# Reordering side work in a hybrid attention and retention layer: stores of f32 rows, operand sums, and the preparation of the output weights

## The chip, the cores and the metric

The kernel runs on one core of a Trainium2 chip. The metric is the device time of one execution in microseconds (us). The engines are TensorE (PE; its weight loads are shown apart as PEld), VectorE (DVE), ScalarE (ACT), GpSimd (POOL) and SyncE (SP), which here only issues DMAs. Each engine works through its own instructions in the order in which they stand in the program.

## What is computed

One layer over 2048 latent tokens and 256 context tokens of width 1024:

```python
h_lat = rmsnorm(x) * norm_g * (1 + scale) + shift        # the same for ctx, with its own scale and shift
na_q, na_k, na_v, na_g, r_q, r_k, r_v, r_g = split(h_lat @ w_in)       # w_in is 1024 x 4096
y_na  = neighbourhood_attention(na_q, na_k, na_v, context k and v, rpb) * silu(na_g)
y_ret = head_rmsnorm(retention(rotary(r_q), rotary(r_k), r_v)) * silu(r_g)
x = x + gate * (concat(y_na, y_ret) @ w_out)             # scale, shift, gate = silu(c) @ w_ada + b_ada
return rmsnorm(x) * final_norm_g
```

All is in f32. The kernel splits each f32 operand into a rounded part ("hi", tiles named hhi, whi) and the rest ("lo", hlo, wlo), and makes one product out of three matmuls: hi x hi, hi x lo, lo x hi.

## The kernel before, in words

The latent tokens are four blocks of 512 (0 to 3), the context is block 4. Weights are taken in columns of 256. The program runs through these stages, one after the other.

**Windows.** `window(b)` for b = 0 to 4 makes the attention keys of block b in 32 steps (a step is three matmuls, or the part of a unit up to its next `yield`). Beside them a table, PLAN, says at which step each piece of the norm and modulation of a later block runs: `squares`, `colsum`, `rstd`, `spread`, `spread_mul` (L241), `prep_ab` (scale and shift in place, L272 and L274) and `prep_hl` (hi on ACT at L279, lo on DVE or POOL at L283). The modulated f32 rows of blocks 0 to 3 are also stored to DRAM, in hS, because blocks 2 and 3 are loaded again later: `prep_hl` puts a pair (i, u) into the list `spill`, and `spill_step` (L253), called at every odd step, issues one store on SP's queue. SP's queue also holds the loads of x (L190), of ctx and of weights (L176) and the stores of the keys kS (L150). An entry of SP that waits holds up what is behind it.

**Context units.** Four units over CTXU (retention k and v of the context), then two for the attention values of the context. A unit is 48 matmuls of 128x256 (L377). Ahead of each, `w_split` (L348 on ACT, L350 on POOL for the first half of the weight and on DVE for the second) splits the weight of the *next* unit.

**First values.** Eight units `u_v` for blocks 0 and 1: each result is copied out of PSUM by ACT (L415) and DVE (L416) and stored by eight DMAs (L425). In the fourth and later units `w_sums` makes the first weights of the stage that follows.

**Round one.** `strassen` over SETS, six column sets for blocks 0 and 1 together, with seven products (L702) in place of eight. Its operands are sums of the blocks' halves (T, made by `h_sums`, ten parts: two each of `first`, `second`, `third`, then four of `fourth`) and sums of the weights' halves (`w_sums`). A set has four `step`s; a list `hooks` of 24 functions gives each step its side work.

**Second values, round two.** The same for blocks 3 and 2: `take` loads their f32 rows from hS into lo tiles (L842), `re_split` makes hi (L519) and lo (L520), and `h_sums_raw` makes the sums: `open_b` first, then nine parts. The units are two of block 3, two of block 3 with the second weight, then four of block 2. The parts of `h_sums` and `h_sums_raw` are not tied to a stage: `unit` pops one from `pump["q"]` after every `pump["every"]` steps.

**Output weights.** The gate row is the sum of eight pieces of w_ada (`wo_gate`, L768 on DVE, one 512 KB load each into `wraw`, L765), spread over the partitions by `wo_row` (four small matmuls, L775). `wo_mul` multiplies half of a 128-row piece of w_out by it (L780 on DVE), splits it (L782 on ACT, L783 on POOL; the tile `g` exists once) and stores both parts to woS from ACT's queue (L785).

**Attention, then retention and the output projection.** Not touched by the change. While attention runs, `fill` puts further projection units (L377, results at L452) between its steps.

What sets the order around the change is thus written by hand: PLAN, the order of appending to `spill`, the numbers of `pump`, and the indices of `hooks`.

Of the kernel before, what the change touches and what calls it, by code (L numbers as in the profile page):

```python
# [82 lines left out]
def hybrid_kernel(ctx: ExitStack, tc: tile.TileContext, a: dict, out: bass.AP):  # L83
# [160 lines left out]
        s, u, q = int(i == 8), k // 2, k % 2  # L244
        return scl[u][:, q, s:s + 1], mod[u][:, 0, q, s:s + 1]

    spill = []

    def spill_step():
        if spill:  # L250
            i, u = spill.pop(0)
            o = i % 2 * 256
            nc.sync.dma_start(hS[i // 2][:, u * KH:(u + 1) * KH, o:o + 256], raw[i][u])  # L253

    def prep_first(k):
        if k == KC - 1:
            spill.extend((i, u) for i in range(2) for u in range(2))
# [18 lines left out]
    def prep_hl(i, u):  # L276
        hi, lo = sub_dst(i)
        x, ks = raw[i][u], slice(u * KH, (u + 1) * KH)
        nc.scalar.copy(hi[:, ks, :], x)  # L279
# [214 lines left out]
    def window(b):  # L494
        units = [u_k(w01, 512 + 256 * g, ct, b) for g in range(2) for ct in range(2)]
        left = [KC] * 4
        for n, u in enumerate(STEPS if b == 0 else [u for u in range(4) for _ in range(KC)]):
            if b == 4 and n == 16:
                wr.append(w_split(wr[2]))
            next(units[u])  # L500
            left[u] -= 1
            run_acts(32 * b + n)
            if n % 2:
                spill_step()
            if not left[u]:
                for _ in units[u]:
                    pass
                tick()
# [16 lines left out]
    def h_sums_raw(T, A, B):  # L525
# [7 lines left out]
        def cast(key, c, d):  # L533
            nc.scalar.copy(t[key][:, 0, pairs(c), :], d)
# [10 lines left out]
            for n in (0, 2, 1, 3):  # L545
                re_split(B, pairs(n), (V, G)[n // 2])

        def a():
            tile_(3, "hlo")
            for c in range(2):  # L550
                cast(3, c, d(c))
            for c in range(2):
                low(3, c, d(c), (V, G)[c])

        def b():
            tile_(2, "hhi")
            for c in range(2):
                V.tensor_tensor(d(c), d(c), xa[:, pairs(c), :], ALU.add)
                cast(2, c, d(c))

        def first(c):
            if c == 0:
                e[0], e[1] = env["st"].tile([P, 2, 512], F32, name="o3", bufs=1), wo["p"].tile([P, 2, 512], F32, name="e")
            V.tensor_tensor(e[c], hb[:, pairs(c), :], xa[:, pairs(c), :], ALU.subtract)
            V.tensor_tensor(e[c], e[c], lb[:, pairs(c), :], ALU.add)
            low(2, c, d(c), (V, G)[c])

        def c_():
            tile_(4, "hlo")
            for c in range(2):  # L570
                V.tensor_tensor(d(c), xa[:, pairs(c + 2), :], d(c), ALU.subtract)
                cast(4, c, d(c))

        def raw_a(m):
            for n in (m, m + 2):
                re_split(A, pairs(n), (V, G)[n // 2])
            low(4, m, d(m), (G, V)[m])

        def last(c):
            if c == 0:  # L580
                tile_(1, "hhi")
                T.extend(t[n] for n in (1, 3, 2, 4))
            cast(1, c, e[c])
            low(1, c, e[c], (V, G)[c])

        return open_b, [a, b, lambda: first(0), lambda: first(1), c_, lambda: raw_a(0), lambda: raw_a(1), lambda: last(0), lambda: last(1)]

    def h_sums(T, A, B):
        (ah, al), (bh, bl) = ((f(x) for x in blk[b]) for b in (A, B))
# [270 lines left out]
    W, mine = values(vunits([(mid, 1024, 3), (w1, 1280, 3), (mid, 1024, 2), (w1, 1280, 2)]),  # L860
                     {0: [lambda: w1.append(w_split(wcur.pop(0), lo=1)), load_w, load_w], 1: [lambda: wo_gate(7)], 7: [wo_row]}, 5)
# [768 lines left out]
```

## Time and profile before

| | us |
|---|---|
| median of three runs | 1410.24 (1408.56 to 1411.27) |
| the profiled execution, whole | 1406.78 |
| its span, first to last instruction | 1405.0 |
| PE busy in the span | 1325.7 (94%) |
| DVE, POOL, ACT busy | 833.4, 654.2, 606.8 |
| mean granted TensorE clock | 0.985 |

The profile is one execution. In its views a row of the timeline gives the start, the duration, the engine, the line, the operation, out<-in by the names of the tiles, the shapes and a count; in brackets stands how long the engine was idle before it, and what ended that. A row of the windows gives, for one stretch of time, the busy time of each engine with the number of its instructions, then the mean granted clock of TensorE (1.00 is full), the share of the DMA engines that was busy, and GB/s. A row of the groups gives the busy time and the mean duration in ns of all instructions of one line and operation.

### The profile page before, as it was taken

The page shows a single profiled execution, that of the slowest core. Times are in us where ns is not written, and L with a number is a line of the kernel's source. Part 1 is how long each engine was busy: PE and PEld are TensorE (multiplying, and loading weights), DVE is VectorE, ACT ScalarE, POOL GpSimd, SP SyncE. Part 2 cuts the span into 40 slices and gives each one's busy share as a digit, 9 for nine tenths or more (in the row PEclk, how much of TensorE's full clock was granted, in tenths as well). Part 3 has the DMA queues.
Part 4 walks back from the last instruction along what each step waited for, and adds up shares of the span by engine and source line. Part 5 has one row for each costly group of instructions (what it writes and reads, how often), then busy time and mean ns, then how long its engine had stood idle before and what let it go on. Part 6 is the DMA issues. An engine that isn't in the chain of part 4 may idle for free.

```text
span 1405.0 us, 23114 instructions
## 1 busy us (share of the span) xinstructions
PE 1325.7 (94%) x8236; PEld 1161.0 (83%) x8236; DVE 833.4 (59%) x1422; ACT 606.8 (43%) x1261; POOL 654.2 (47%) x603
## 2 busy tenths in 40 slices
PE   6988979999879999899999999899999999999997
PEld 2567979988778878898899899798999779888886
DVE  5786364466673656267766777677663543344445
ACT  5453332233343344265556455565562234333332
POOL 4451445355444566355355455656343155454342
PEclk9999989999989999999999999999999999999999
DMA  9685636654655566895776788857636998555433
GB/s 320 206 275 190 207 123 172 159 186 152 247 160 138 189 241 218 256 242 162 203 195 198 187 253 209 212 159 204 174 114 214 272 309 270 187 171 168 157 113 128
DMA packets 233301, 278.86 MB, mean 198 GB/s; under 512 B 17121, under 2 KB 180065, under 8 KB 232162
## 3 DMA queue, kind: packets, MB, share of 16 engines
q1 hardware_dynamic: 201858, 221.01, 54.3%
q10 hardware_dynamic: 31328, 56.37, 11.1%
q8 instruction: 66, 1.08, 0.3%
q14 instruction: 49, 0.40, 0.1%
HBM read 188.19 MB, written 89.13 MB: 197 GB/s over the span
## 4 chain that ended last, share of the span: by engine, by line
PE 65%; DMA 8%; DVE 8%; POOL 7%; issue 6%; ACT 4%; SPq 2%; ACTq 1%; POOLq 0%; DVEq 0%
PE mm L377 16%; PE mm L1474 11%; PE mm L702 10%; PE mm L366 7%; PE sS L1034 4%; PE tr L1061 3%; PE po L1082 3%; PE mm L1197 2%; DMA hlo<-hS 2%; PE tr L1063 2%; PE po L1084 1%; DMA woS<-g 1%; PE mm L314 1%; POOL hlo L520 1%; DMA v<-rvS 1%
## 5 line engine op out<-in xcount | busy, mean ns | idle before, releaser
L377 PE MATMUL mm<-whi,hhi 128*128 128x256 f32 x768 | 227.6, 296 | 8.3 <-ACT hhi L519 4.6
L377 PE MATMUL mm<-whi,hlo 128*128 128x256 f32 x768 | 220.5, 287 | 8.2 <-DVE hlo L520 5.7
L377 PE MATMUL mm<-wlo,hhi 128*128 128x256 f32 x768 | 219.9, 286 | 1.6 <-POOL wlo L350 1.6
L1065 ACT CAST pt<-tr 128x640 fp32r<-128x640 f32 (+1 forms) x128 | 95.7, 747 | 162.4 <-PE tr L1063 156.9
L1071 DVE TENSOR_TENSOR pt<-tr,pt 128x640 fp32r<-128x640 f32 (+1 forms) x128 | 113.9, 890 | 80.5 <-ACT pt L1065 79.3
L377 PEld LDWEIGHTS mm<-whi,hlo 128*128 128x128 f32 x768 | 149.7, 195 | 9.6 <-DVE hlo L520 6.6
L377 PEld LDWEIGHTS mm<-whi,hhi 128*128 128x128 f32 x768 | 149.4, 194 | 9.2 <-ACT hhi L519 5.2
L1054 POOL TENSOR_SCALAR sp<-sp,stt 128x640 f32<-128x640 f32 (+2 forms) x128 | 103.1, 808 | 107.9 <-DVE stt L1053 78.4
L377 PEld LDWEIGHTS mm<-wlo,hhi 128*128 128x128 f32 x768 | 149.3, 194 | 1.8 <-POOL wlo L350 1.8
L1043 DVE CUSTOM_DVE_ANT_0 sp<-sS,nb 128x640 f32<-128x640 f32 (+2 forms) x128 | 105.5, 824 | 36.2 <-PE sS L1034 29.6
L1048 ACT ACTIVATE sp<-sp,stt 128x640 f32<-128x640 f32 (+2 forms) x128 | 107.4, 839 | 20.7 <-DVE stt L1043 19.6
L350 POOL TENSOR_TENSOR wlo<-st,whi 128x256 fp32r<-128x256 f32 (+1 forms) x79 | 83.6, 1069 | 59.2 <-ACT whi L348 48.3
L366 PE MATMUL mm<-hhi,whi 128*128 128x512 f32 x256 | 107.7, 421 | 0.0
L366 PE MATMUL mm<-hlo,whi 128*128 128x512 f32 x256 | 101.5, 397 | 5.6 <-DVE hlo L283 2.3
L1034 PE MATMUL sS<-k,q 128*128 128x256 f32 (+3 forms) x512 | 99.1, 315 | 5.8 <-DVE stt L1043 5.6
L366 PE MATMUL mm<-hhi,wlo 128*128 128x512 f32 x256 | 101.7, 397 | 0.2 <-DVE wlo L350 0.2
L702 PE MATMUL mm<-hhi,whi 128*128 128x512 f32 x336 | 98.4, 395 | 1.5 <-POOL whi L656 1.3
L1474 PE MATMUL mm<-wor,y 128*128 128x512 f32 x384 | 95.7, 398 | 1.2 <-DVE xt L1483 1.1
L1483 DVE TENSOR_TENSOR xt<-mm,xt 128x512 f32<-128x512 f32 x64 | 43.8, 686 | 84.7 <-PE mm L1474 84.6
L1034 PEld LDWEIGHTS sS<-k,q 128*128 128x128 f32 x512 | 82.7, 188 | 12.8 <-DVE stt L1043 9.1
L1474 PE MATMUL mm<-won,y 128*128 128x512 f32 x336 | 89.9, 406 | 0.0
L656 POOL TENSOR_TENSOR wlo<-st,wlo 128x512 fp32r<-128x512 f32 x36 | 51.5, 1432 | 79.7 <-ACT wlo L655 74.9
(274 smaller groups left out, 3159.3 us busy)
## 6 DMA issues: line engine op xcount, KB each, us to landing
st<-in_w_in_dram SPq DMA_DIRECT2D x64, 512.0 KB, 6.4
q<-qS SPq DMA_DIRECT2D x64, 256.0 KB, 4.4
k<-kS SPq DMA_DIRECT2D x16, 576.0 KB, 9.3
kS<-o SPq DMA_DIRECT2D x16, 512.0 KB, 3.5
vB<-o SPq DMA_DIRECT2D x64, 128.0 KB, 2.1
qS<-o ACTq DMA_DIRECT2D x16, 512.0 KB, 6.2
hlo<-hS SPq DMA_DIRECT2D x16, 512.0 KB, 7.7
woS<-g ACTq DMA_DIRECT2D x32, 256.0 KB, 3.3
```

The lines of the kernel that those rows point to most:

```text
L350: eng.tensor_tensor(l, r, f(h), ALU.subtract)
L366: nc.tensor.matmul(pm[:, :n], ww[:, k, cs], h[:, k, :], start=(k == 0 and i == 0), stop=(k == KC - 1 and i == 2))
L377: nc.tensor.matmul(pm[:, t * WG:(t + 1) * WG], h[:, k, o:o + P], ww[:, k, :], start=(k == 0 and i == 0), stop=(k == KC - 1 and i == 2))
L656: nc.gpsimd.tensor_tensor(t[:, 1], r, f(t)[:, 0], ALU.subtract)
L702: nc.tensor.matmul(pm, ww[:, k, :], hh[:, k, :], start=(k == 0 and i == 0), stop=(k == KH - 1 and i == 2))
L1034: nc.tensor.matmul(o, hd["q"][i][:, hl, j * P:(j + 1) * P], k, start=(hl == 0), stop=(hl == 1))
L1043: nc.vector.tensor_tensor_reduce(T["sp"][:, :n], T["s"], nbz[big][:, o:o + n], -1.0, 3e38, ALU.add, ALU.min, T["st"][:, 0:1])
L1048: nc.scalar.activation(sp[:, :n], sp[:, :n], AF.Exp, bias=st[:, 0:1], scale=-1.0, accum_out=st[:, 1:2])
L1054: nc.gpsimd.tensor_scalar(sp[:, :n], sp[:, :n], st[:, 2:3], 0.0, ALU.mult, ALU.add)
L1065: nc.scalar.copy(pt[:, :ng_ + 2, 0, :], tr[:, :ng_ + 2, :])
L1071: nc.vector.tensor_tensor(pt[:, :n, 1, :], tr[:, :n, :], f(pt)[:, :n, 0, :], ALU.subtract)
L1474: nc.tensor.matmul(pm, yy[:, k, :], ww[:, k, sl], start=(k == 0 and i == 0), stop=(k == 3 and i == 2))
```

## The change

Five things, all of order; the arithmetic of the outputs is the same.

1. An entry of `spill` carries the step from which it may go, eight steps after it was made; `spill_step(n)` leaves it where n is smaller.
2. `h_sums` for blocks 0 and 1 goes into the pump after the last weight split of the context units, and a part is popped every 6 steps in place of 8. The first part falls into the first attention-value unit of the context, the last into the sixth of the eight value units.
3. `h_sums_raw` is cut into ten parts. All sums that read f32 rows of block 2 come first (`p2`, `p3`, `p4`), then the split of block 2 (`p5` twice), then the casts and low parts of the sums (`p7`, `p8`, `p10`). `d4` has a place of its own, where `d` was overwritten. The pump starts one step earlier.
4. `open_b`, which holds the split of block 3, moves from the third step of round one's last set to the second.
5. All eight `wo_gate` run in round one, at every second step; `wo_row` runs at the end of its fifth set. Of the sixteen `wo_mul` four run in the second values, and twelve at every second step of round two, where sixteen stood in 24 steps.

```diff
-    spill = []
-    def spill_step():
-        if spill:
-            i, u = spill.pop(0)
+    spill, now = [], [0]
+    def spill_step(n):
+        if spill and spill[0][2] <= n:
+            i, u, _ = spill.pop(0)
...
-            spill.append((i, u))
+            spill.append((i, u, now[0] + 8))
...
-    pump["q"] = h_sums(T, 0, 1)
     for c0, u in CTXU:
         wn = w_split(wcur.pop(0), lo=1)
         load_w()
         unit(u(w0, c0, 8))
         w0 = wn
     w1 = w_split(wcur.pop(0), lo=1)
     load_w()
+    pump.update(y=0, every=6, q=h_sums(T, 0, 1))
     for w, c0 in ((w0, 1024), (w1, 1280)):
         unit(u_v(w, c0, 8))
...
-    for k in range(7):
-        hooks[3 * k + 2].append(lambda k=k: wo_gate(k))
+    for k in range(8):
+        hooks[2 * k + 1].append(lambda k=k: wo_gate(k))
+    hooks[19].append(wo_row)
+    halves = [lambda k=k, n=n: wo_mul(k, n) for k in range(8) for n in range(2)]
     hooks[20].insert(0, lambda: take(3))
     hooks[21].insert(0, take_a)
-    hooks[22].append(lambda: raws[0]())
+    hooks[21].append(lambda: raws[0]())
...
-    pump.update(y=2, every=4, q=raws[1])
+    pump.update(y=3, every=4, q=raws[1])
-                     {0: [...], 1: [lambda: wo_gate(7)], 7: [wo_row]}, 5)
+                     {0: [...], **{n: [halves.pop(0)] for n in (1, 3, 5, 7)}}, 5)
...
-    for k in range(8):
-        for n in range(2):
-            hooks[3 * k + n].append(lambda k=k, n=n: wo_mul(k, n))
+    for n in range(12):
+        hooks[2 * n].append(halves.pop(0))
```

The parts of `h_sums_raw`, where `low` is the lo part of one sum, on DVE (V) or POOL (G), and `xa` are the f32 rows of block 2:

```python
p1:  cast(3, 0), cast(3, 1); low(3, 0) on V, low(3, 1) on G
p2:  d(c) = d(c) + xa[c]                 # before: with cast(2, c) right behind each
p3:  d4(c) = xa[c + 2] - d(c)            # before: after the sums e, with cast(4, c) right behind each
p4:  e[c] = hb[c] - xa[c]
p5(m): re_split(block 2, m on V, m + 2 on G)          # m = 0, then 1
p7:  casts and lows of d4;  p8: of d;  p9: e[c] += lb[c];  p10: casts and lows of e
```

Three places show how the instructions move. First, SP's queue in the windows, rows with - as before and with + as changed (hS_87 to hS_90 are the stores of the f32 rows of blocks 0 to 3, kS the stores of keys, chi and clo the tiles of the last two parts of x):

```order
+L150 DMA kS_64<-o 256x1x512
 L253 DMA hS_89<-hhi 128x4x256 x3
-L150 DMA kS_64<-o 256x1x512
 L150 DMA kS_61<-o 256x1x512
-L253 DMA hS_90<-chi 128x4x256 x2
 L176 DMA st<-in_ctxT_dram 128x4x256 x2
 L150 DMA kS_62<-o 256x1x512
+L253 DMA hS_90<-chi 128x4x256 x2
 L150 DMA kS_63<-o 256x1x512
```

The two stores from chi stood ahead of the load of the context and stand behind it now, and behind one more store of keys. The last three stores of block 2's rows have the key store kS_64 in front of them now, where it stood behind them.

Second, DVE in the context units (wlo is the lo part of a weight, hhi and hlo in these rows are tiles of the first pair's sums, o<-mm the copy of a unit's result out of PSUM). Before:

```order
L387 TENSOR_TENSOR o<-mm,o 128x256 x4
L350 TENSOR_TENSOR wlo<-st,whi 128x1024
L608 TENSOR_TENSOR hhi<-hhi 128x1024
L610 TENSOR_TENSOR hhi<-hhi 128x1024
L600 TENSOR_TENSOR hlo<-hhi,hlo 128x1024
```

Changed (its L620, L622 and L612 are L608, L610 and L600 of before):

```order
L387 TENSOR_TENSOR o<-mm,o 128x256 x4
L350 TENSOR_TENSOR wlo<-st,whi 128x1024 x5
L620 TENSOR_TENSOR hhi<-hhi 128x1024
L622 TENSOR_TENSOR hhi<-hhi 128x1024
L612 TENSOR_TENSOR hlo<-hhi,hlo 128x1024
L416 TENSOR_TENSOR o<-mm,o 128x4x128
```

The five weight splits, which had the parts of the sums between them, stand together; the sums come behind the last.

Third, ACT in the second values, from the first casts of the sums on (L415 copies a value unit's result, L348 splits the second value weight, L519 is the hi part of block 2, L534 the hi part of a sum). Before:

```order
L534 CAST hlo<-hhi 128x1024 x2
L534 CAST hhi<-hhi 128x1024 x2
L415 CAST o<-mm 128x4x2x64
L348 CAST whi<-st 128x1024 x2
L415 CAST o<-mm 128x4x2x64
L534 CAST hlo<-hhi 128x1024 x2
L519 CAST hhi<-hlo 128x1024 x2
L415 CAST o<-mm 128x4x2x64
L519 CAST hhi<-hlo 128x1024 x2
```

Changed (L535 and L520 are L534 and L519 of before, L794 is L782):

```order
L535 CAST hlo<-hhi 128x1024 x2
L415 CAST o<-mm 128x4x2x64
L348 CAST whi<-st 128x1024 x2
L415 CAST o<-mm 128x4x2x64
L794 CAST g<-wraw 128x512
L520 CAST hhi<-hlo 128x1024 x4
L415 CAST o<-mm 128x4x2x64
L535 CAST hlo<-hhi 128x1024 x2
```

The hi part of block 2 stood behind three pairs of casts of the sums and now stands behind one, but also behind a cast of the output weights.

More of the change, by code (lines that the diff above doesn't have):

```diff
@@ L256, in prep_first @@
         if k == KC - 1:
-            spill.extend((i, u) for i in range(2) for u in range(2))
+            spill.extend((i, u, now[0] + 8) for i in range(2) for u in range(2))
         for i in range(2):
@@ L551, in a, with p2 @@
                 cast(3, c, d(c))
[L552 to L556, printed above, removed]
+            low(3, 0, d(0), V)
+            low(3, 1, d(1), G)
+        def p2():
             for c in range(2):
                 V.tensor_tensor(d(c), d(c), xa[:, pairs(c), :], ALU.add)
[L559 to L566, printed above, removed]
@@ L575, in raw_a, with p5, both @@
+        def p5(m):
             for n in (m, m + 2):
                 re_split(A, pairs(n), (V, G)[n // 2])
[L577 to L586, printed above, removed]
+        def both(key, src, first):
+            for c in range(2):
+                cast(key, c, src(c))
+            for c in range(2):
+                low(key, c, src(c), (V, G)[c ^ first])
@@ new lines, in p7, with p8, p9, p10 @@
+        def p7():
+            tile_(4, "hlo")
+            both(4, d4, 1)
+        def p8():
+            tile_(2, "hhi")
+            both(2, d, 0)
+        def p9():
+            for c in range(2):
+                V.tensor_tensor(e[c], e[c], lb[:, pairs(c), :], ALU.add)
+        def p10():
+            tile_(1, "hhi")
+            T.extend(t[n] for n in (1, 3, 2, 4))
+            both(1, lambda c: e[c], 1)
+        return open_b, [p1, p2, p3, p4, lambda: p5(0), lambda: p5(1), p7, p8, p9, p10]
```

21 lines of the change are left out of this document (12 added, 9 removed).

## The prediction

> **What bounds the kernel now.** I read the page first, then the windows by stage, then each stage's rows by engine.
>
> ```profile
> PE 1325.7 (94%) x8236; PEld 1161.0 (83%) x8236; DVE 833.4 (59%) x1422; ACT 606.8 (43%) x1261; POOL 654.2 (47%) x603
> ```
>
> TensorE is the bound, so the change can only win back time in which it idles or runs at a lower clock. The windows, cut at the stages' borders, tell where that is:
>
> ```profile
> 82.00:131.00 49.00, 41.47 (x182) 32.79 (x182) 37.92 (x54) 23.92 (x33) 17.38 (x13) 0.97 0.69 233
> 166.50:263.70 97.20, 87.95 (x673) 86.71 (x672) 53.76 (x43) 27.54 (x38) 45.52 (x24) 0.93 0.56 160
> 263.70:380.40 116.70, 116.64 (x504) 94.40 (x503) 71.00 (x83) 40.70 (x70) 55.86 (x39) 1.00 0.55 188
> 380.40:448.00 67.60, 53.29 (x383) 51.61 (x384) 43.90 (x33) 23.87 (x30) 30.32 (x12) 0.87 0.58 158
> 448.00:582.40 134.40, 131.79 (x607) 106.58 (x605) 77.38 (x95) 52.74 (x90) 78.19 (x56) 1.00 0.64 211
> 582.40:601.00 18.60, 14.86 (x112) 14.83 (x112) 0.73 (x2) 5.15 (x8) 6.27 (x8) 0.91 0.94 291
> ```
>
> A stage's loss is its length less PE's busy time, plus length times (1 - clock). The windows stage (82 to 131) loses 7.5 + 1.5 = 9.0 us, the context units with the first values 9.3 + 6.8 = 16.1, round one nothing, the second values 14.3 + 8.8 = 23.1, round two 2.6, the start of attention 3.7 + 1.7 = 5.4. The change touches these stages alone; all they lose is 56 us, which no gain can pass.
>
> **Part 1, the spill stores.** PE's longest wait in the windows stage is for the context's squares:
>
> ```profile
> 105.28 4.99 SPq L150 DMA_DIRECT2D kS<-o  x2
> 112.01 4.16 SPq L253 DMA_DIRECT2D hS<-chi  x2
> 116.27 1.55 SPq L176 DMA_DIRECT2D st<-in_ctxT_dram  x2
> 112.06 1.05 ACT L279 CAST hhi<-chi 128x1024 fp32r<-128x1024 f32 x1
> 117.26 1.09 ACT L274 ACTIVATE clo<-clo,mods 128x256 f32<-128x256 f32 x2
> 121.46 1.06 ACT L198 ACTIVATE st<-st 128x1024 f32<-128x1024 f32 x1 [3.10 <-DMA st<-in_ctxT_dram]
> 126.34 0.24 PE L209 MATMUL mm<-one,st 128*128 128x1 f32 x1 [4.17 <-DVE st L203]
> hS<-hhi SPq DMA_DIRECT2D x8, 512.0 KB, 5.2
> ```
>
> The context's load waits on SP behind two stores that wait for their rows. Moved ahead of them it issues at about 110.3, 6 us sooner. What is late next is ACT: its L274 pair ends at 118.35, so the two L198 end at 120.5 in place of 124.0, and DVE, which has scaling of clo until about 121.1, comes 2.9 sooner. So 4.17 shrinks to about 1.3. Against that, the last three hS stores of block 2 now stand behind a key store and issue from 105.9 to 107; with 5.2 us to land they free their buffer near 112.3, and ACT's L279 of 112.06, which writes there, may slip by some 0.5. Half of the clock loss may go. I take **3.0**, range 0 (the slip takes it) to 4.5 (all of this wait and its clock).
>
> **Part 2, the first sums.** What the context units wait for:
>
> ```profile
> 170.19 3.39 POOL L609 TENSOR_TENSOR hhi<-hlo 128x1024 f32<-128x1024 f32 x1
> 171.24 3.42 DVE L608 TENSOR_TENSOR hhi<-hhi 128x1024 f32<-128x1024 f32 x1
> 176.02 1.05 ACT L599 CAST hlo<-hhi 128x1024 fp32r<-128x1024 f32 x1 [7.31 <-DVE hhi L610]
> 177.47 1.98 ACT L348 CAST whi<-st 128x1024 fp32r<-128x1024 f32 x2
> 178.58 2.35 POOL L350 TENSOR_TENSOR wlo<-st,whi 128x1024 fp32r<-128x1024 f32 x1 [5.00 <-ACT whi L348]
> 180.98 0.49 PE L377 MATMUL mm<-wlo,chi 128*128 128x256 f32 x1 [1.93 <-POOL wlo L350]
> 246.47 0.59 ACT L415 CAST o<-mm 128x512 fp32r<-128x512 f32 x1 [4.13 <-DMA vB<-o]
> 252.19 0.59 ACT L415 CAST o<-mm 128x512 fp32r<-128x512 f32 x1 [4.61 <-DMA vB<-o]
> ```
>
> ACT sits on a sum's cast until DVE has the sum; the weight's casts stand behind it, and PE waits. Without the sums a split starts when the unit before it has been copied out (0.6), then 1.05 of ACT and 2.35 of POOL: 4.0 us, under the 5.72 of a unit (the distance of the last two rows). The second half, on DVE, comes about 1.2 after POOL's and is needed only at 7. So the stage's 16.1 go, if the sums fit beside the ten units that are left, 57 us. Their rows:
>
> ```profile
> L608 DVE TENSOR_TENSOR hhi<-hhi 128x1024 f32<-128x1024 f32 x2 | 6.8, 3409 | 0.0
> L610 DVE TENSOR_TENSOR hhi<-hhi 128x1024 f32<-128x1024 f32 x2 | 2.5, 1226 | 0.2
> L600 POOL TENSOR_TENSOR hhi<-hhi 128x1024 fp32r<-128x1024 f32 x2 | 4.8, 2400 | 9.3 <-ACT hhi L599 9.3
> L638 POOL TENSOR_TENSOR e<-hlo 128x512 f32<-128x512 f32 x4 | 7.0, 1744 | 0.0
> L600 POOL TENSOR_TENSOR hhi<-o,hhi 128x512 fp32r<-128x512 f32 x4 | 5.2, 1294 | 5.8 <-ACT hhi L599 5.8
> ```
>
> At 170.19 POOL and DVE each took longer than their rows when alone (2.40 and 1.23) and ended one after the other, at 173.58 and 174.66: on such operands I let them run in turn. From the end of the last context unit but two the chain is: 5 us of weight split; `first` 2 x 7 (2.4 + 1.2 + 1.2, ACT 1.05, DVE 1.2); `second` and `third` 4 x about 5, partly overlapped; `fourth` 4 x 4.4; the weight sums 6; DVE's ten copies in between. Walked through by hand, the weight part that the third product needs is ready at 64.6 after that point, and PE reaches it at 62.7; DVE's copies lag by up to 13 us, some three units, which the six PSUM tiles cover. So about 2 us come back: **14**, range 8 to 16.1.
>
> **Part 3, the second pair's sums and the split of block 3.**
>
> ```profile
> 379.49 2.35 DVE L544 TENSOR_TENSOR hhi<-hlo 128x1024 f32<-128x1024 f32 x2
> 381.76 4.53 DVE L520 TENSOR_TENSOR hlo<-hlo,hhi 128x1024 fp32r<-128x1024 f32 x2
> 411.25 2.35 DVE L571 TENSOR_TENSOR hhi<-hlo,hhi 128x1024 f32<-128x1024 f32 x2
> 412.50 2.18 ACT L534 CAST hlo<-hhi 128x1024 fp32r<-128x1024 f32 x2 [13.23 <-DVE hhi L571]
> 415.68 0.38 PE L377 MATMUL mm<-whi,hhi 128*128 128x256 f32 x1 [3.76 <-ACT hhi L519]
> 425.77 0.39 PE L377 MATMUL mm<-whi,hlo 128*128 128x256 f32 x1 [2.59 <-POOL hlo L520]
> ```
>
> Block 3's split stood behind the last set's sums on DVE; one step earlier it starts when the reload lands, about 375.5, four us sooner. DVE's copies of that set then wait behind it for some 5 us, which PSUM holds. The DVE and POOL parts in turn end at 382.7 and 385, so PE still waits some 2.5 us at the start (4.0 before). The second weight's split is no longer behind two casts that wait for DVE, but POOL has a low part in front of it: 1.2 (1.6 before). Block 2's split waits for one thing on ACT, the cast of the output weights, which waits for DVE to reach L780; counted from row to row DVE is there at 402.7, the last low part is done at 411.6, and PE, which reaches block 2 at 407, waits about 3 (8.9 before). Sum 6.7 of idle, and two half-clock stretches, 3.4: of 23.1 lost 10.1 stay. **13**, range 5 (block 2 as late as before) to 20.
>
> By the Trainium skill's TensorE: Matmul & The Clock Gate, HAM oscillation, what hurts is idling for more than about 3.4 us. Here a wait of 1.93 us (row of 180.98) was enough for a matmul of 0.49 behind it, so the trace does not bear that bound out; by it the waits left in the second values would cost no clock, and this part would be 16.4.
>
> **Part 4, the output weights.** Round two's 2.6 and the start of attention:
>
> ```profile
> 580.22 0.62 ACT L782 CAST g<-wraw 128x512 fp32r<-128x512 f32 x1 [6.30 <-DMA woS<-g]
> 585.54 0.58 ACT L452 COPY o<-mm 128x512 f32<-128x512 f32 x1
> 586.17 0.39 PE L377 MATMUL mm<-whi,hhi 128*128 128x256 f32 x1 [3.75 <-ACT o L452]
> 600.08 0.72 DVE L1043 CUSTOM_DVE_ANT_0 sp<-sS,nb 128x544 f32<-128x544 f32 x1 [23.51 <-PE sS L1034]
> ```
>
> ACT waits for the single tile g to be stored, and the projection's copy-out waits behind it. With halves two steps (some 9.7 us) apart the store has landed. Both waits go; but DMA is 0.94 busy from 582 to 601, and attention's first scores may then wait for their loads. I take 2.3 + 3.2 = **5.5**, range 1 to 8. The gate row costs nothing: eight sums beside products on a DVE that is busy 71 of 117 us, and the four matmuls only change place.
>
> **Sum.** 3.0 + 14 + 13 + 5.5 = 35.5 us. The profiled execution took 1406.78 (span 1405.0, 1.8 around it): 1371.3. It lies 3.5 under the median of the three runs, so beside that median I forecast 1410.2 - 35.5 = **1375 us**. All lower ends together give 14, so 1396; all upper ends 48.6, so 1362.
>
> **The rivals.**
>
> *A, the first sums come late* (chance 11%). If DVE and POOL run strictly in turn and the ACT casts and copies between them (about 16 us) hide nothing, the 58 us of turns (DVE 26, POOL 32) become 74 from 4 us on, and the third product waits 15 us in place of 2, with 7 of clock: 1375 + 20 = 1395. For it: the rows of 170.19 and 171.24. Against: in those rows ACT works while the others do. The Trainium skill has it so too: SBUF — State Buffer, Who interferes with whom, makes the port pair of VectorE and GpSimd an exclusive lock for a whole instruction.
>
> *B, the same place, slower than before* (4%). If every large operation there takes its longest duration (3.4 for 128x1024, 1.75 for 128x512) and no two overlap, ten parts take 29 + 45 + 30, the weight sums 16, the copies 13: 133 us in 58. PE then waits some 75 at the start of round one: 1450. It decides from a lateness of 37 us on. Against it: L610 and L600 took 1.23 and 2.40.
>
> *C, loads set the pace of the context units* (9%). Each unit needs 1 MB; at 160 GB/s that is 6.5 us, over 5.72. Then part 2 gives 6: 1383. Against: 291 GB/s in the last window, with 0.94 of DMA.
>
> *D, block 2 is late as before* (14%), since ACT's cast of g is a new wait in front of it and DVE is the one behind both. Part 3 gives 5: 1383.
>
> **How the numbers follow.** The forecast has 62%, with a range of its own of 1362 to 1390. A, C and D are still faster by over 0.2% (2.8 us, about what a measurement of this kernel can tell from no change), but for 3 points of A's tail. Faster 0.93, same 0.03, slower 0.04. The range 1361 to 1396 leaves out B and the tails.
>
> **What would show it.** Right: the two stores from chi behind the context's load and PE's wait at L209 near 1 us; no wait of PE for wlo in the context units and clock 1.00 there; a wait under 3 us at the third product of round one; in the second values under 8 us of idle; no wait for L452 at the start of attention. Wrong: an idle PE at the start of round one (A, B), ACT's L348 waiting for DMA (C), ACT's L519 waiting behind the cast of g (D), or new waits in attention, which I take as untouched.

## The result and the profile after

The changed kernel takes **1390.05 us** (median of 4 runs, 1388.99 to 1393.31) against 1410.76 for the kernel before (4 runs, 1408.56 to 1415.97): a ratio of 0.985, 95% interval 0.982 to 0.988. The forecast was 1375 with a range of 1361 to 1396. The sign and the range held, the range at its upper end; of the 35.5 us forecast some 21 came. The profiled execution took 1390.82 (span 1388.9), 16 less than that of before.

The page of the changed kernel, engines:

```profile
PE 1320.5 (95%) x8236; PEld 1152.0 (83%) x8236; DVE 841.9 (61%) x1422; ACT 606.8 (44%) x1261; POOL 655.0 (47%) x603
```

The windows of the changed kernel, cut at the first and last products of each stage (columns as in the prediction: length, busy time of PE, PEld, DVE, ACT, POOL, granted clock, DMA share, GB/s):

```profile
82.00:131.00 49.00, 45.57 (x210) 36.27 (x209) 38.59 (x57) 25.49 (x37) 17.77 (x13) 1.00 0.81 268
162.50:243.12 80.62, 80.62 (x674) 80.62 (x673) 47.31 (x33) 25.02 (x33) 40.01 (x20) 1.00 0.55 161
243.12:374.79 131.67, 124.36 (x511) 97.90 (x509) 82.30 (x92) 47.45 (x80) 64.91 (x46) 0.96 0.58 193
374.79:430.17 55.38, 48.72 (x385) 47.59 (x384) 44.54 (x32) 21.48 (x28) 28.75 (x12) 0.97 0.62 174
430.17:558.03 127.86, 120.36 (x508) 95.22 (x507) 77.07 (x91) 48.72 (x84) 75.39 (x55) 0.99 0.66 215
558.03:580.88 22.85, 22.85 (x192) 22.85 (x192) 4.23 (x7) 6.12 (x9) 7.10 (x8) 1.00 0.95 280
```

The context units with the first values (second row) and the start of attention (last) lose nothing any more: PE is busy for the whole length at full clock. Round one (third row), which lost nothing before, now loses 7.3 us of idle time and 4% of its clock. Stage by stage, with both traces cut at the same products:

| stage | before | after | gained | forecast |
|---|---|---|---|---|
| up to the windows' first product | 28.15 | 29.19 | -1.0 | 0 |
| windows | 138.10 | 133.31 | 4.8 | 3.0 |
| context units and first values | 97.26 | 80.62 | 16.6 | 16.1 |
| round one | 116.82 | 131.67 | **-14.9** | **-2.1** |
| second values | 69.11 | 55.38 | 13.7 | 13 |
| round two | 121.48 | 127.86 | **-6.4** | **+2.3** |
| start of attention | 28.36 | 22.85 | 5.5 | 3.2 |
| all behind it | 805.72 | 808.07 | -2.3 | 0 |

So the stages that were to gain did so, and two stages behind them gave back 21 us where the forecast had a balance of 0. (1.7 of round one's 14.9 are the gate row's four matmuls, which stood in the second values before.) What PE waits for there, by the timeline of PE in the changed kernel (start, duration, instruction, idle time before it and what ended it):

```profile
251.76 0.50 PE L714 MATMUL mm<-hhi,wlo 128*128 128x512 f32 x1 [3.01 <-ACT wlo L667]
253.78 1.22 PE L714 MATMUL mm<-hhi,wlo 128*128 128x512 f32 x2 [1.10 <-POOL wlo L668]
283.48 0.73 PE L714 MATMUL mm<-hhi,whi 128*128 128x512 f32 x2 [1.03 <-ACT whi L667]
285.55 1.91 PE L714 MATMUL mm<-hhi,whi 128*128 128x512 f32 x5 [1.34 <-POOL whi L668]
439.08 0.50 PE L714 MATMUL mm<-hhi,wlo 128*128 128x512 f32 x1 [3.28 <-ACT wlo L667]
460.01 0.47 PE L714 MATMUL mm<-hhi,whi 128*128 128x512 f32 x1 [1.73 <-DVE o L750]
```

The weights of a set's seven products are called, in the order of their use, a11, a12, s4, a22, s2, s3 and s1; the tiles of s4 and a22 are named wlo, those of a11, a12, s2 and s3 whi. ACT's L667 casts the hi part of each, POOL's L668 makes the lo part. Both rounds wait at their third product, s4, and again in their second set. For the first set of round one, ACT's timeline has the reason:

```profile
185.74 0.59 ACT L452 COPY o<-mm 128x512 f32<-128x512 f32 x1 [2.67 <-PE mm L377]
250.09 0.62 ACT L611 CAST hhi<-o 128x512 fp32r<-128x512 f32 x1 [6.35 <-DVE o L652]
250.61 0.58 ACT L415 CAST o<-mm 128x512 fp32r<-128x512 f32 x1
251.09 0.62 ACT L667 CAST wlo<-st 128x512 fp32r<-128x512 f32 x1
258.43 0.58 ACT L415 CAST o<-mm 128x512 fp32r<-128x512 f32 x1 [6.24 <-DMA vB<-o]
258.92 1.14 ACT L667 CAST whi<-st 128x512 fp32r<-128x512 f32 x2
```

s4's cast (251.09) stands behind the cast of the last part of the sums, which waits 6.35 for DVE. The casts of s3 and s2 (258.92) stand behind the copy-out of the last value unit, which waits 6.24 for its o tile to be stored. That copy comes 15 us after PE ended the unit (243.12, the border of the windows), and what is still to be copied and cast is what round one starts with. In the second set ACT casts s3 and s2 (282.29) behind its L723, which waits 3.97 for DVE, and DVE waits there for a store of the round's own results:

```profile
279.75 0.69 DVE L760 TENSOR_TENSOR o<-mm,e 128x512 f32<-128x512 f32 x1 [3.91 <-DMA qS<-o]
280.48 0.63 ACT L723 ACTIVATE o<-o 128x512 fp32r<-128x512 f32 x1 [3.97 <-DVE o L760]
```

### The profile page after: what moved, and what is told of

Same layout as the page of the kernel before. It is cut to its first block, busy times and chain, and to the rows that moved or that the text cites. A ratio compares the mean times of both kernels' runs of the same rounds, so it can differ in the third digit from the quotient of the medians.

```text
span 1388.9 us, 23101 instructions
## 1 busy us (share of the span) xinstructions
PE 1320.5 (95%) x8236; PEld 1152.0 (83%) x8236; DVE 841.9 (61%) x1422; ACT 606.8 (44%) x1261; POOL 655.0 (47%) x603
## 4 chain that ended last, share of the span: by engine, by line
PE 63%; DVE 12%; DMA 8%; issue 6%; POOL 4%; ACT 4%; SPq 3%; ACTq 0%; DVEq 0%; POOLq 0%
PE mm L377 13%; PE mm L1487 11%; PE mm L714 11%; PE mm L366 7%; PE sS L1047 4%; PE tr L1074 3%; PE po L1095 3%; DMA vB<-o 2%; PE mm L1210 2%; PE mm L314 2%; PE tr L1076 2%; PE po L1097 1%; SPq L425 1%; DMA v<-rvS 1%; PE mm L1399 1%
## 5 line engine op out<-in xcount | busy, mean ns | idle before, releaser
L377 PE MATMUL mm<-whi,hhi 128*128 128x256 f32 x768 | 224.7, 293 | 0.0
L377 PE MATMUL mm<-whi,hlo 128*128 128x256 f32 x768 | 217.7, 284 | 4.9 <-DVE hlo L521 4.3
L714 PE MATMUL mm<-hhi,whi 128*128 128x512 f32 x336 | 100.2, 401 | 4.7 <-POOL whi L668 2.0
L668 POOL TENSOR_TENSOR wlo<-st,wlo 128x512 fp32r<-128x512 f32 x36 | 52.0, 1444 | 69.3 <-ACT wlo L667 69.3
```

The lines of the kernel that those rows point to most:

```text
L377: nc.tensor.matmul(pm[:, t * WG:(t + 1) * WG], h[:, k, o:o + P], ww[:, k, :], start=(k == 0 and i == 0), stop=(k == KC - 1 and i == 2))
L668: nc.gpsimd.tensor_tensor(t[:, 1], r, f(t)[:, 0], ALU.subtract)
L714: nc.tensor.matmul(pm, ww[:, k, :], hh[:, k, :], start=(k == 0 and i == 0), stop=(k == KH - 1 and i == 2))
```

## The experiments

Theories, as the expectations name them:

- *1*: the first sums end too late, and the weights of round one are late with them; *1a* by the order of the instructions on ACT and DVE, *1b* because DVE and POOL take turns, so that the chain through both is the bound.
- *2a*: the gate row's sums, now in round one, keep DVE from catching up; *2b*: the output weights' halves (the calls of `wo_mul`) beside the last second values stand in front of round two's s4.
- *3*: the two o tiles and their vB stores, all on one queue, hold up ACT.

All runs are against the kernel before on the same chip (medians 1409.3 to 1411.1). Medians of two variants 2 us apart are inside their intervals, so stages are compared as well: where the code of a stage was as in the changed kernel, its length repeated within 0.1 us (context units and first values), 1.3 (second values) and 2.7 (round two).

**The first sums back beside the context units.**

```
     T = []
+    pump["q"] = h_sums(T, 0, 1)
     for c0, u in CTXU:
...
-    pump.update(y=0, every=6, q=h_sums(T, 0, 1))
```

> The changed kernel with the first pair's sums back beside the context units (every eighth product step from the start); all else as changed. In the changed kernel the context units and the first values ran 16.6 us shorter than before, but round one lost 12.2 us that it did not lose before (7.1 of idle, 5.1 of clock), beside the 1.7 of the gate row's matmuls, which only moved there. Theory 1 (the sums end too late, and weight sums, copy-outs and stores pile up at round one's start): both go together, the 16.6 are lost again and the 12.2 come back; 1390 + 4 = 1394, between 1392 and 1397, and no wait of PE in the first 45 us of round one. Theory 2 (the gate row's eight sums, moved closer together into round one, hold DVE up there): only the 16.6 are lost; 1406, and round one keeps its waits. Theory 3 (the vB stores, all on one queue, keep the o tiles): as theory 1 in the time, but PE's waits in the second set of round one stay.

1391.38 us (ratio 0.9872, 0.9848 to 0.9896). Windows of this run, the context units with the first values, and round one:

```profile
161.81:257.58 95.77, 86.66 (x675) 85.42 (x674) 53.77 (x43) 27.50 (x38) 45.71 (x24) 0.95 0.57 162
257.58:376.12 118.54, 118.54 (x511) 95.53 (x509) 72.24 (x82) 44.84 (x74) 58.27 (x41) 1.00 0.57 193
```

The first stage loses 15.2 again, and round one, with the gate row still in it, loses nothing. So the part moved the loss from one stage to the next: 15.2 gained, 131.67 - 118.54 = 13.1 lost. The traces keep 2 us of it; the medians of the two kernels, 1391.38 and 1390.05, don't tell them apart. The gate row as a cause of its own (theory 2a, in the expectation theory 2) fell here: it costs its four matmuls (118.54 - 116.82 = 1.7) and no wait when the sums are out of the way.

**The gate row and the output weights at their old places.**

```
-    for k in range(8):
-        hooks[2 * k + 1].append(lambda k=k: wo_gate(k))
-    hooks[19].append(wo_row)
+    for k in range(7):
+        hooks[3 * k + 2].append(lambda k=k: wo_gate(k))
...
-                     **{n: [halves.pop(0)] for n in (1, 3, 5, 7)}
+                     1: [lambda: wo_gate(7)], 7: [wo_row]
...
-    for n in range(12):
-        hooks[2 * n].append(halves.pop(0))
+    for k in range(8):
+        for n in range(2):
+            hooks[3 * k + n].append(halves.pop(0))
```

> The changed kernel with the gate row and the output weights back at their places of before: gate sums at every third step of round one, the last of them and the row's matmuls in the second values, the halves at two of three steps of round two. Theory 1 (first sums end too late): round one keeps its loss of 12.2 us, less the 1.7 of matmuls that leave it; the projection's wait at the start of attention (5.5) is back; round two gives back what the halves cost it: 1390 + 0 to + 6. Theory 2 (the gate row in round one holds DVE up): round one's loss goes, 10 to 12 us; 1380 to 1385 with the attention's start lost. Theory 3 (stores): as theory 1.

1388.69 us (0.9845, 0.9819 to 0.9872). Windows of round one, second values, round two, start of attention:

```profile
241.94:368.18 126.24, 121.21 (x507) 96.06 (x505) 83.00 (x91) 46.45 (x78) 67.35 (x46) 0.97 0.59 194
368.18:424.86 56.68, 50.24 (x389) 48.40 (x388) 46.02 (x33) 20.88 (x27) 27.03 (x11) 0.97 0.63 177
424.86:548.67 123.81, 119.75 (x508) 94.27 (x507) 77.39 (x91) 49.57 (x85) 74.34 (x54) 1.00 0.64 215
548.67:577.64 28.97, 24.64 (x193) 24.44 (x192) 5.29 (x9) 6.58 (x10) 8.29 (x9) 0.94 0.91 270
```

The projection's wait is back (6.1 longer), but round two is 4.1 shorter, and round one 5.4, 1.7 of it the row's matmuls: together 335.7 against 337.8. So by this trace the new places of the gate row and the weights cost about 2 us instead of gaining 5.5; these 2 are inside what the stages differ by, the 4.1 of round two are not. Round one's wait at its third product was the same (3.01 and 0.80), as theory 1 has it, and the total is far from theory 2's 1380 to 1385; the waits of its second set are gone. The gate sums cost 3.7 there only behind the late sums: with the sums at their old place they cost no wait.

**Gate sums at steps 8 to 15.**

```
-        hooks[2 * k + 1].append(lambda k=k: wo_gate(k))
+        hooks[k + 8].append(lambda k=k: wo_gate(k))
```

> The changed kernel with the gate row's eight sums at steps 8 to 15 of round one in place of every other step from the first; all else as changed. Theory 2a (the gate sums in the first two sets keep DVE from catching up with what the first sums left over): the waits at 277 to 286 go (3.0 of idle, 1.7 of clock), 1385; the wait at 252 stays, since no gate sum is ahead of it. Theory 1: the waits in the second set come from the late start alone and stay, 1388 to 1391. Eight sums of 1.28 us in eight steps of five could make new waits in the third and fourth set, up to 3 us.

1388.93 us (0.9844, 0.9821 to 0.9867). The waits at 277 to 286 fell from 3.0 to 0.4, as theory 2a says, but the second part of s2 in the first set came 1.34 late (0.21 before), and other waits came in the fourth and fifth set. PE's timeline:

```profile
252.07 0.80 PE L714 MATMUL mm<-hhi,wlo 128*128 128x512 f32 x1 [4.24 <-ACT wlo L667]
323.64 0.72 PE L714 MATMUL mm<-hhi,whi 128*128 128x512 f32 x2 [1.68 <-POOL whi L668]
346.21 0.50 PE L714 MATMUL mm<-hhi,whi 128*128 128x512 f32 x1 [1.81 <-POOL whi L668]
```

Round one took 133.4: one cost at another place.

**Two halves in the second values in place of four.**

```
-                     **{n: [halves.pop(0)] for n in (1, 3, 5, 7)}
+                     **{n: [halves.pop(0)] for n in (1, 3)}
...
-    for n in range(12):
-        hooks[2 * n].append(halves.pop(0))
+    for k in range(7):
+        for n in range(2):
+            hooks[3 * k + n].append(halves.pop(0))
```

> The changed kernel with two of the output weights' halves in the second values (beside the second and the fourth unit) in place of four, and the other fourteen at two of three steps of round two. Theory 2b (the halves beside the last units of the second values stand in front of s4's cast): the wait of 3.3 and 0.6 us at the third product of round two goes, with 1.7 of clock, and so does what follows in its second set (3.2); round two 127.9 to about 122, 1384. Theory 1 (round two starts late for the ten sums in the second values, not for the halves): the wait stays, 1388 to 1391. The wait for L452 at the start of attention should stay away either way, since the last half is at step 19; if it is back, 5.5 are lost.

1389.39 us (0.9855, 0.9828 to 0.9882). The wait of 3.28 at s4 was 1.40 here and those of the second set were gone, but round two got further waits of 0.2 to 1.3 from its third set on and took 128.7, so nothing was gained. That s4 waits for the halves (2b) is not shown by it: a later run with the same code there (all three edits) waited 2.85 at s4. The projection did not wait.

**The low difference issued one part ahead.** `low_diff(k)` is POOL's line L650 for part k; that of part 0 stands ahead of these lines.

```
             V(d, bh[:, k, :], ah[:, k, :], ALU.subtract)
             V(d, d, e, ALU.add)
+            if k + 1 < KH:
+                low_diff(k + 1)
```

> The changed kernel with one edit in the last four parts of the first sums: POOL's difference for the next part is issued ahead of POOL's low part of this one, so DVE no longer waits for it (1.2, 2.7 and 3.7 us in the changed kernel) and ACT's cast no longer for DVE. Theory 1 (the sums end too late): the weight part that the third product waits for is ready 4 to 7 us sooner, the wait of 4.1 us at 252 and its half clock of 3.4 go, and some of the second set's 3.0 and 1.7; 1390 - 7 to - 12, 1378 to 1383. Theory 2 (gate row): no change, 1388 to 1391. Theory 3 (the stores' queue): the first wait goes but the o tiles are kept as long, and the second set's waits stay: 1382 to 1384. If DVE and POOL only take turns, so that the sum of their work is the bound, nothing is gained: 1389 to 1391.

1385.97 us (0.9829, 0.9802 to 0.9856). The waits at the third product fell from 3.01 and 1.10 to 1.89 and 1.29; round one took 130.2, only 1.4 less. DVE waited less for POOL, but its instructions took longer: 52.9 us of DVE in the context units and first values in place of 47.3. The weight sums that stand in front of the last part on DVE began about 2.5 us sooner and ended only 1.0 sooner. The total lies between the forecasts of theory 1 (1378 to 1383) and of strict turns (1389 to 1391) and decides for neither.

**A part at every fifth step.** `every=6` becomes `every=5`.

> The changed kernel with the first sums' parts at every fifth product step in place of every sixth, so that the last part stands two value units ahead of the weight sums of s4 and not between them. Theory 1a (the order on ACT: s4's cast stands behind the cast of the last part, which waits for DVE, 6.4 us in the changed kernel): s4 is split some 5 us sooner, the wait of 4.1 at 252 and its 3.4 of clock go, and the set after it is less late; 1390 - 7 to - 12, 1378 to 1383. Theory 1b (DVE and POOL only take turns, 56 of 63 us with at least one of them busy, so the order is worth little): the same waits, 1387 to 1391, with the value units' copy-outs later by what the sums are sooner.

1387.81 us (0.984, 0.9815 to 0.9865); the wait at the third product was 3.05, the second one there gone, but 0.36 and 1.33 came at s2, and round one took 131.9. Order alone was worth about nothing, as 1b says.

**Both of these edits.**

> The changed kernel with two edits that each gave 2 to 4 us alone: the low difference of the next part issued ahead of POOL's low part of this one, and a part at every fifth product step. In the first alone s4's cast still stood behind the weight sums of DVE, which had the last part behind them; in the second alone behind the last part's wait for POOL. Theory 1a (order): together they bring s4 some 6 us sooner, PE's wait of 3 to 4 us at 250 and its clock go: 1379 to 1382. Theory 1b (turns): 1384 to 1388, no more than the larger of the two.

1385.68 us (0.9827, 0.9812 to 0.9842). PE's timeline in this run (L718 and L671 are L714 and L667):

```profile
250.71 0.73 PE L718 MATMUL mm<-hhi,wlo 128*128 128x512 f32 x2 [0.62 <-POOL wlo L672]
258.21 0.73 PE L718 MATMUL mm<-hhi,whi 128*128 128x512 f32 x2 [2.14 <-ACT whi L671]
260.28 2.08 PE L718 MATMUL mm<-hhi,whi 128*128 128x512 f32 x4 [1.33 <-POOL whi L672]
```

The wait for s4 is gone, and a wait of 2.14 and 1.33 for s3 and s2 stands in its place, which the first wait had hidden. Round one took 128.9: 3.5 of the 4.1 us at s4 went, and 3.5 came back 7 us later.

**The low parts of the first sums on DVE.**

```
-            (V if key == 3 else G)(t[:, 1, ks, :], d, f(t)[:, 0, ks, :], ALU.subtract)
+            V(t[:, 1, ks, :], d, f(t)[:, 0, ks, :], ALU.subtract)
-            G(e, bl[:, k, :], al[:, k, :], ALU.subtract)
+            V(e, bl[:, k, :], al[:, k, :], ALU.subtract)
```

> The changed kernel with all low parts of the first sums, and the last four parts' low differences, on DVE in place of POOL. Alone, such a part takes DVE 1.23 (128x1024) or 0.69 us (128x512) and POOL 2.4 or 1.3. Theory 1b (DVE and POOL take turns and the chain through both of them is the bound): four parts of 1.2 and eight of 0.6 are saved, and with them the hand-overs between the two (1.2 to 3.7 us at each of the last four parts), 10 us or more; s4's weights are in time, the waits at 252 (4.1, and 3.4 of clock) and in the second set (3.0 and 1.7) go: 1390 - 8 to - 13, 1377 to 1382. Rival (the two work side by side, and DVE, with 44 of 63 us busy, is the bound): DVE gets 10.4 us more, the copy-outs come later, and round one loses 5 more, 1395. Theory 3 (the value units' own chain of two o tiles and eight stores each sets the pace, whatever the sums do): 1387 to 1391.

1386.71 us (0.9834, 0.9815 to 0.9854). The same sum on DVE, first in the changed kernel, where POOL works at a low part,

```profile
211.03 5.85 POOL L612 TENSOR_TENSOR hhi<-hhi 128x1024 fp32r<-128x1024 f32 x2 [14.01 <-ACT hhi L611]
214.56 3.41 DVE L639 TENSOR_TENSOR hhi<-hhi 128x1024 f32<-128x1024 f32 x1
```

then in this run, where POOL has nothing to do:

```profile
218.44 1.22 DVE L639 TENSOR_TENSOR hhi<-hhi 128x1024 f32<-128x1024 f32 x1
251.07 0.72 PE L714 MATMUL mm<-hhi,wlo 128*128 128x512 f32 x2 [0.62 <-POOL wlo L668]
258.46 0.73 PE L714 MATMUL mm<-hhi,whi 128*128 128x512 f32 x2 [2.05 <-ACT whi L667]
```

With more work on DVE (55.1 us in the context units and first values in place of 47.3), s4 is ready sooner: 0.62 of wait in place of 4.1. So DVE as a full engine is not the bound, and for s4 1b holds: what counts is the chain through DVE and POOL, in which each waits for the other. How much of it is POOL's slower pace and how much the turns was not told apart. The total is not 1b's (1377 to 1382), though: a wait for s3 and s2 stands behind it, as in the run with both edits, and round one took 129.2, only 2.4 less.

**Half of the vB stores from ACT's queue.**

```
-                defer(1 + r, lambda dst=dst[r], src=o[64 * r + k0:64 * r + k0 + cw]: nc.sync.dma_start(dst, src))
+                defer(1 + r, lambda dst=dst[r], src=o[64 * r + k0:64 * r + k0 + cw],
+                      q=nc.scalar if e % 2 and tp < 4 else nc.sync: q.dma_start(dst, src))
```

> The changed kernel with half of the first values' vB stores issued from ACT's queue in place of SP's. Theory 3 (the one queue keeps the two o tiles): ACT's wait of 6.2 us and DVE's of 3.1 for vB<-o after 252 go, the second set's weight casts come some 6 us sooner, and its waits (3.0 of idle, 1.7 of clock) are gone: 1385, or 1382 if the first wait shrinks as well. Theory 1 (the sums end too late): the wait of 4.1 us at 252 and its half clock stay, the second set gains at most its own 4.7: 1385 to 1390. Theory 2: no change, 1388 to 1391. Against all of it, 16 more issues of 0.37 us on ACT can make its casts later, up to 3 us.

1389.23 us (0.9852, 0.9827 to 0.9877). The waits of the second set went, but s4's grew to 5.87, since ACT stood at its stores until DVE had written its half of the o tile, and 0.55 and 1.33 came at s2; round one 131.1. No gain: theory 3 names a wait that is there, but not one that this takes away. As ACT now waits for its own stores, the run does not tell what the one queue alone costs.

**Three edits together:** every fifth step, halves apart, gate sums later.

> The three edits together: first sums at every fifth step, two halves in the second values and fourteen in round two, gate sums at steps 8 to 15. If theories 1a, 2a and 2b all hold: round one loses nothing, round two about 3 in place of 9; 1390 - 12 - 6, about 1372. If 1b holds in place of 1a: 1390 - 5 - 6, 1379. If none of them holds: 1388 to 1391.

1388.79 us (0.9846, 0.9818 to 0.9873), round one 131.2, round two 126.4: nothing of the 11 to 18 expected.

**Sums on DVE, every fifth step, gate sums at every third step.** Beside the two edits shown:

```
-        hooks[2 * k + 1].append(lambda k=k: wo_gate(k))
-    hooks[19].append(wo_row)
+        hooks[(2, 5, 8, 11, 14, 17, 20, 21)[k]].append(lambda k=k: wo_gate(k))
+    hooks[22].append(wo_row)
```

> Sums on DVE as in the run above, a part at every fifth step, and the gate sums at every third step of round one (2, 5, ... 20, 21), its row at step 22. By theory 1b round one loses nothing at its start (12 us less), and by theory 2a the second set gets DVE back, 1376 to 1380; round two keeps its loss of 9. By theory 3 or with DVE as the bound: 1387 to 1395.

1385.19 us (0.9833, 0.9816 to 0.985). Round one took 125.4, 6.3 less, with the waits for s3 and s2 (1.92 and 1.38) still there and none in the second set. Still the total is over the 1376 to 1380 of 1b and 2a together. Round two and the second values took 2.3 more in this trace; in the next run, with the same code there, they took 0.5 less than in the changed kernel, so the 2.3 are no effect of the edits.

**The same with s3's and s2's casts ahead of the last value unit.**

```
-            if at <= n < at + 3:
+            if at <= n < at + 4:
                 mine[n - at]()
...
-        mine[3]()
+        if at + 3 >= len(vu):
+            mine[3]()
```

> The kernel with the sums on DVE, parts at every fifth step and the gate sums at every third step of round one, with one edit more: the casts of s3 and s2 are issued ahead of the first values' last unit, not behind its copy-out. In the kernel without the edit these casts stand on ACT behind that copy-out, which waits 3.1 us for its o tile's vB stores, and TensorE waits 1.9 and 1.4 us for them at 258 (the wait at the third product is 0.6 there already). Theory 3 in its last form (once the sums are in time, the o tiles are what the weights wait for): both waits and 1.7 of clock go, 1385 - 3 to - 5, 1380 to 1382. Rival (ACT and DVE as a whole are behind at that point, and the wait moves to the next weights): 1384 to 1386, with a wait of 2 to 3 us in the second set in its place.

**1383.73 us** (1382.60 to 1386.97; ratio 0.9814, 0.9793 to 0.9835), below every run of the changed kernel; against the run without this edit (0.9833) the intervals overlap. Round one of this run, and PE's timeline behind its start:

```profile
243.40:368.41 125.01, 120.38 (x511) 94.79 (x509) 80.86 (x91) 46.97 (x78) 61.79 (x43) 1.00 0.62 204
```

```profile
250.17 0.73 PE L714 MATMUL mm<-hhi,wlo 128*128 128x512 f32 x2 [0.62 <-POOL wlo L668]
267.77 0.47 PE L714 MATMUL mm<-hhi,whi 128*128 128x512 f32 x1 [1.03 <-DVE o L750]
271.69 0.50 PE L714 MATMUL mm<-hhi,wlo 128*128 128x512 f32 x1 [0.92 <-ACT wlo L667]
273.58 0.73 PE L714 MATMUL mm<-hhi,wlo 128*128 128x512 f32 x2 [1.16 <-POOL wlo L668]
```

The two waits at 258 are gone, but 3.1 us of new ones stand in the second set. This is the wait that the rival of the expectation names: the place was right, and yet ACT and DVE are behind as a whole, so that the wait moves on. The time lies just under the rival's 1384 to 1386. The clock stays at 1.00, and round one loses 125.0 - 118.5 = 6.5 in place of 13.1; in the run without the edit it was 125.4, so the edit alone is worth nothing that these runs can tell.

## Why the prediction was right, and where it was wrong

**The number.** Sign, range and most of the mechanisms held, but that the time lies in the range is in part luck. 1390.05 is at the very edge of the 1362 to 1390 that the forecast itself had. By the stages part 2 came out at 16.6 - 13.1 = 3.5 where its range was 8 to 16.1, and part 4 at 5.5 - 6.4 = -0.9 where its range was 1 to 8; parts 1 and 3, at 4.8 and 12.0, made up for it.

**What bounds the kernel** held: PE's waits and the clock behind them were what moved, and the limit of 56 us was not touched.

**Part 1** was right in its mechanism: 4.8 in place of 3.0. The difference tells little, since this stage took from 131.1 to 135.6 in the runs, with the same code. On SP the context's load now goes ahead of the chi stores, and PE's wait at L209 fell from 4.17 to 0.19; I had left 1.3. The slip that I feared is there, 1.23 of ACT at L279, and costs PE nothing. Rows of SP, ACT and PE in the changed kernel:

```profile
112.19 2.69 SPq L176 DMA_DIRECT2D st<-in_ctxT_dram  x2
115.01 1.05 ACT L279 CAST hhi<-chi 128x1024 fp32r<-128x1024 f32 x1 [1.23 <-DMA hS<-hhi]
120.85 1.58 SPq L253 DMA_DIRECT2D hS<-chi  x2
124.15 0.58 PE L209 MATMUL mm<-one,st 128*128 128x1 f32 x4 [0.19 <-DVE st L203]
```

**Part 2** was wrong in its size, and this is most of the miss. That the context units' 16.1 go was right (16.6). The step that failed is "So about 2 us come back": 13.1 came back. The row of ACT at 185.74 is the end of the last context unit but two; from there s4's half was ready at 253.72 (POOL's L668, 252.01 and 1.71 long), that is 68.0, where the walk by hand had 64.6, and PE was there at 63.0 (62.7). So the walk itself was off by only 3.4 us. What it left out is the price of being late: 4.1 of idle at s4, 3.4 of clock behind it (6.8 us at half clock), and a backlog that made the second set wait 3.0 and 1.7 of clock more. These make 12.2 of the 13.1; 3.7 of it came only with the gate row behind the late sums (part 4). So the part is worth 2 us by the run with the sums back, and 3.5 by the stages, not 14. The walk stopped at the first late product; the value copies that were "up to 13 us" late did not stop PE, as it said, but they stood on ACT in front of the next weights.

**Part 3** was right in its steps: 3.1 of idle at the start (2.5), 1.8 at the second weight (1.2), and 1.8 at block 2 where I had 3, 6.7 in sum as forecast. Its gain, 13.7 less the 1.7 of the row's matmuls that left the stage, is 12.0 against 13, and that is so near because two errors cancel. The rule for a stage's loss counts idle time at low clock twice. PE needs 47.4 for this stage at clock 1.00 (run with the sums back), so 69.1 - 1.7 - 47.4 = 20.0 were lost before and not 23.1; and 55.4 - 47.4 = 7.9 stay and not 10.1, since one stretch at half clock was left and not two. The 16.4 named beside the 13, with no clock lost at all, did not come: the wait of 2.33 was followed by half clock. PE's rows at the first and the last of these:

```profile
378.96 0.58 PE L377 MATMUL mm<-whi,hlo 128*128 128x256 f32 x1 [2.33 <-DVE hlo L521]
407.06 0.38 PE L377 MATMUL mm<-whi,hlo 128*128 128x256 f32 x1 [1.27 <-DVE hlo L521]
```

**Part 4** had the right mechanism at the start of attention: no wait for L452, and all of that stage's loss went (5.5 against 3.2); DMA at 0.95 did not hold the scores up. Two steps failed. "Both waits go" for round two: it lost 6.4 more instead of gaining 2.3. With the old places 4.1 of that did not come, and PE waited neither at s4 nor in the second set. The waits of the second set come from a load: DVE stands 8.0 us at a half for its piece of w_out, whose load SP issues behind 32 stores of vB, and the L750 that PE waits for at 460.01 follows on DVE.

```profile
421.12 25.86 SPq L425 DMA_DIRECT2D vB<-o  x32
447.08 0.36 SPq L777 DMA_DIRECT2D wraw<-in_w_out_dram  x1
452.46 0.69 DVE L792 TENSOR_TENSOR wraw<-wraw,gacc 128x512 f32<-128x512 f32 x1 [7.97 <-DMA wraw<-in_w_out_dram]
```

In the two runs with two halves beside the second values DVE has no such wait there, and PE none in the second set. What makes s4 late was not told apart: ACT casts it behind the copy-out of the last value unit, which waits 4.11 for a vB store; with the old places that copy waited 3.32 but came 6 us sooner in the round. The other step that failed is "the gate row costs nothing": with DVE behind after the first sums, it cost 3.7. Against the old places the part gains nothing (2 us of loss by the trace, which the spread does not tell from none).

**The rivals.** C and D did not happen: PE ran at 1.00 through the context units, and block 2 waited 1.8. B did not either. A, at 11%, had the mechanism: DVE and POOL in turn, a late s4, half clock behind it. It put 15 us on that wait where 4.1 came, and 7 on the clock where 3.4 came, but its total of 22 is nearer to the 13 that were lost than the 2 of the forecast. Behind the start of attention 2.3 us were lost with no edit there; that part of the kernel differed by up to 6.8 us between traces of variants with the same code in it, so nothing can be read from it.

## What to carry to other kernels

Work that is moved out of one stage's waits ends later, and its price at the border had three terms here: the idle time of the first late product, the clock behind it, and the backlog on the in-order engines that makes the next weights late; walk on until the backlog is gone, not to the first late product. Where several things are late at one point, taking one away shows the next, so count what each is worth only with all of them gone. Of a step that is free beside idle engines, ask what it costs when the step ahead has left them behind.

## What the runs showed of the hardware

A DVE sum of 128x1024 took 3.41 us while POOL worked at its own part and 1.22 when POOL was idle; the long one ended at 217.97, 1.09 after POOL's. By the Trainium skill's SBUF — State Buffer, Who interferes with whom, the two engines share a port pair under an exclusive lock; these rows agree with it.

The same wait of 2.33 us at the same instruction was followed by half clock in one execution and not in another. In the changed kernel the granted clock was 0.56 from 379.00 to 382.20, and a product took 0.42:

```profile
379.33 0.42 PE L377 MATMUL mm<-wlo,hhi 128*128 128x256 f32 x1
```

In the run with the first sums back at the context units it was 1.00 from 380.30 to 383.50, and a product took 0.28:

```profile
380.28 0.39 PE L377 MATMUL mm<-whi,hlo 128*128 128x256 f32 x1 [2.33 <-DVE hlo L521]
380.50 0.28 PE L377 MATMUL mm<-wlo,hhi 128*128 128x256 f32 x1
```

Over the second values the clock was 0.97 in the one and 1.00 in the other, and PE's busy time 48.72 and 47.44 us. What decides it is not in these traces.
